# An mLSTM stage re-laid: outputs' pool at the other end of SBUF, more buffers, the first head's keys read in place, the next head's weights split ahead of the output gate

## The chip, the cores and the metric

One core of a Trainium2 chip runs the whole layer in one launch. The metric is the device time of an execution in microseconds (us); runs of one kernel are compared by their median. TensorE (PE) does the matmuls, VectorE (DVE) and ScalarE (ACT) the work on their results, GpSimd (POOL) some of it on SBUF, and SyncE (SP) issues most transfers. SBUF is shared by tiles that the program names; PSUM holds matmul results in banks.

## The reference

One layer of a diffusion backbone on 1024 latent tokens and 256 context tokens, width 1024. Only the part that matters here:

```python
h, hc = modulated RMS norms of x and ctx
aq, ak, av, mq, mk, mv, mo, mg, ga, gm = split_in_proj(h @ w_in)      # and the same of hc
att = windowed_gqa(q, k, v, k_ctx, v_ctx, sink)                       # branch B, 16 heads
ht = mlstm_bidirectional(mq, mk, mv, gates, ...context...)            # branch A, 4 heads
#   per head, chunks of 128 tokens, both directions (context first):
#   C = decay*C + (k*wk)^T v ;  h = (S v + q C*w) / max(|nq|, exp(-m)),  S = (q k^T)*exp(dmat)
ml = rms_norm(ht, norm_w) * sigmoid(mo)
y = (sigmoid(ga) * (att @ w_ba) + sigmoid(gm) * (ml @ w_bm)) @ w_out
x = x_mid + g2 * conv_ffn(norm(x_mid))
```

## The kernel before, in words

The work has four stages, one after another: start-up (modulation, context projections, `hT`, the normalized tokens transposed), attention with the branch gates, the mLSTM, and the tail (branch products, output projection, ConvFFN). Matmuls are made from fp16 or fp32r pieces: an operand is split into a high and a low half (`split_from`: ACT writes the high half, DVE the rest), and three products are summed (`mm3`, lines L163 to L165). Weights are scaled first: their squares are summed on ACT, added up by a small matmul with ones (L119), turned into a factor on POOL (L121, L122), and then split (`split_from`).

**Order of the work.** Each engine, and each engine's queue of transfers, runs its instructions in a fixed order. In attention the order is written out by hand (`tc.manual_schedule()`); elsewhere a planner orders the instructions of each engine by program order, by its own costs and by when it thinks that buffers come free. Work of a later stage is moved up into an earlier one where its inputs and its buffers allow. `tc.issue_after(x)` puts an instruction behind x on x's engine. Pools lie in SBUF as two stacks, one from each end (`side="right"` is the upper end); with `reuse_waits="tile"` a tile waits only for the earlier tiles that lay in its own bytes.

**End of attention.** In the last iterations PE makes the first mLSTM head's key and value products of the eight latent blocks (`early`), and `early_act` copies each from PSUM to `E.kv0[j]` (128x384, fp32, in the pool `kv0` at the upper end). POOL splits the weights of the first head there.

**mLSTM.** `prepare(h)` loads and squares head h's two weights, `load_kv(h)` splits the key/value weight (`whkv` on ACT, `wlkv` on DVE, L56). `proj_kv(h)` makes k and v of ten blocks (two of the context from DRAM tiles `vr`, eight of latent tokens): ACT copies the key (`k`), writes the value's high half (`VH`) and squares all 384 columns with an accumulator (`kvj`, L1325, into `sq`), DVE writes `VL`. `trans_k` transposes the keys on PE (`kT`, L1370) and splits them (`kh`, `kl`). `proj_q` does the queries (`qh`, `ql`, `qj`). `states(h)` turns the sum of squares into a scale (`mlq`, L1435), and updates the states of both directions: `kwh` on POOL, `kwl` on DVE, the product `dC` on PE, the sum `C` on DVE. `masked` adds the masks to the gate rows (`ub`, L1414; POOL for the first head, DVE for others), `decays` takes their exponentials on ACT (L1424). `core(h)` makes S, scales it by `ub` (L1485), splits it (`sh`, `sl`), and then per chunk and direction the outputs `o` and `i`, which go through `nm` (L1503 to L1508) into `hf`. `proj_o(h)` makes the output gate's products (`mo`, `sg`), `readout(h)` the norm, `turn(h)` transposes `hf` (`mt`, L1548), gates it and stores it (`mlT_d`, L1551). `branch_sums` prepares sums of tail weights (`s_ba` and others) in tiles of the outputs' pool `rp`.

The pool `rp` (`sg`, `hf`, `mo`, `kvj`, `qj`, about 22 KB of each partition) is the last of the lower stack. The tail opens its pools over the same lower stack from its bottom up; the first operands of the branch products are the weights `bawr` and the attention outputs `baar` (L1745), split into `bawh`, `bawl`, `baah`, `baal`. The gate rows `sga` (L1776) lie at the upper end.

The order of the calls in `stage_mlstm`:

```python
load_kv(0); proj_q(0); proj_kv(0)
E.kvx.close()
trans_k(0); states(0); masked(0); decays(0, nullcontext())
for _ in range(2): branch_sums()
for h in range(MLH):
    core(h); proj_o(h); readout(h)
    if h + 1 < MLH:
        prepare(h + 1); load_kv(h + 1); masked(h + 1)
        proj_kv(h + 1); trans_k(h + 1); proj_q(h + 1); states(h + 1)
```

Of the kernel before, what the change touches and what calls it, by code (L numbers as in the profile page):

```python
# [8 lines left out]
F32 = mybir.dt.float32  # L9
F32R = mybir.dt.float32r  # L10
F16 = mybir.dt.float16
BF16 = mybir.dt.bfloat16
AF = mybir.ActivationFunctionType
# [5 lines left out]
P = 128  # L19
# [6 lines left out]
NCB = NCTX // P  # L26
NBLK = NT // P
# [4 lines left out]
DQK = 128  # L32
# [13 lines left out]
def copy_act(nc, out, in_, scale=1.0):  # L46
    return nc.scalar.activation(out, in_, AF.Copy, scale=scale)  # L47
# [124 lines left out]
@with_exitstack  # L172
def layer_kernel(ctx: ExitStack, tc: tile.TileContext, A: dict, out: bass.AP, dbg=None):
    nc = tc.nc
    dbg = dbg or {}

    cp = ctx.enter_context(tc.tile_pool(name="cp", bufs=1, reuse_waits="tile"))
    dr = ctx.enter_context(tc.tile_pool(name="dr", bufs=1, space=DRAM, reuse_waits="tile"))

    ident = cp.tile([P, P], F32, name="ident")  # L180
    nc.sync.dma_start(ident, A["ident"])
    expo = cp.tile([P, 16], F32, name="expo")
    nc.gpsimd.memset(expo, -0.5)

    attT_d = dr.tile([D, L], F32, name="attT_d")
    mlT_d = dr.tile([D, L], F32, name="mlT_d")
    sga_d = dr.tile([D, L], F32, name="sga_d")
    sgm_d = dr.tile([D, L], F32, name="sgm_d")


    vecT = cp.tile([P, 256], F32, name="vecT")
    V_C, V_N1, V_N2, V_BM, V_CB, V_CW = 0, 16, 24, 32, 80, 124
    mods = cp.tile([P, 4, KT], F32, name="mods")
    m2 = cp.tile([P, 3, KT], F32, name="m2")
    g_d = [dr.tile([1, D], F32, name=f"g{i}_d") for i in range(2)]
    sil = cp.tile([P, KT, 2], F32, name="sil")

    psx = ExitStack()
    ps1 = psx.enter_context(tc.tile_pool(name="ps_mm", bufs=2, space=PSUM, reuse_waits="tile"))
    psx_t, psx_s = ExitStack(), ExitStack()  # L200
    banks = {}

    def turn_banks(n):
        psx_s.close()
        psx_t.close()
        banks["tp"] = psx_t.enter_context(tc.tile_pool(name=f"ps_tp{n}", bufs=n, space=PSUM, reuse_waits="tile"))

    def score_banks(n):
        banks["s"] = psx_s.enter_context(tc.tile_pool(name=f"ps_s{n}", bufs=n, space=PSUM, reuse_waits="tile"))

    turn_banks(3)
    score_banks(1)
    ph1 = ExitStack()
    hp = ph1.enter_context(tc.tile_pool(name="hTp", bufs=1, reuse_waits="tile"))
    hH = [hp.tile([P, L], F16, name=f"hH{k}") for k in range(KT)]
    hL = [hp.tile([P, L], F16, name=f"hL{k}") for k in range(KT)]
    hT = list(zip(hH, hL))
    gtile = hp.tile([P, NBLK, 16], F32, name="gtile")
    gb = hp.tile([P, 16], F32, name="gb")

    def mm_tile(name):
        return ps1.tile([P, 512], F32, tag="mm", name=name)

    def fl_tile(name):
        return ps1.tile([P, 512], F32, tag="fl", name=name, bufs=1)

    def tp_tile(name):
        return banks["tp"].tile([P, 512], F32, tag="tp", name=name)

    def s_tile(name):  # L230
        return banks["s"].tile([P, 1024], F32, tag="s", name=name)

    kx_d = dr.tile([NCB, P, MLH * DQK], F32, name="kx_d")
    vx_d = dr.tile([NCB, P, MLH * DV], F32, name="vx_d")
    E = Ctx()
    E.__dict__.update(
        nc=nc, tc=tc, A=A, ident=ident, expo=expo, vecT=vecT, mods=mods, m2=m2, g_d=g_d, maccs={}, hT=hT, gtile=gtile, gb=gb, dr=dr, out=out,
        attT_d=attT_d, mlT_d=mlT_d, sga_d=sga_d, sgm_d=sgm_d, kx_d=kx_d, vx_d=vx_d, sil3=sil, sil=sil[:, :, 0], dbg=dbg,
        mm_tile=mm_tile, fl_tile=fl_tile, tp_tile=tp_tile, s_tile=s_tile, psx_s=psx_s, turn_banks=turn_banks, score_banks=score_banks,
    )  # L240
    E.ones = cp.tile([P, P], F32, name="ones")
    nc.gpsimd.memset(E.ones, 1.0)
    E.hs = cp.tile([P, 2], F32, name="hs")
    E.w2 = ScaledWeights(E, tc, ph1)
    with ExitStack() as st:
        at = attention_setup(E, st)
        stage_startup(E, at)
        if dbg.get("stop") != "hT":
            stage_attention(E, st, at)
    if "attT" in dbg:  # L250
        dump(nc, tc, attT_d, dbg["attT"])
    if "sga" in dbg:
        dump(nc, tc, sga_d, dbg["sga"])
        dump(nc, tc, sgm_d, dbg["sgm"])
    if dbg.get("stop") in ("hT", "att"):
        ph1.close()
        psx_t.close()
        psx.close()
        return
    with ExitStack() as st:  # L260
        stage_mlstm(E, st)
    if "mlT" in dbg:
        dump(nc, tc, mlT_d, dbg["mlT"])
    E.gcx.close()
    ph1.close()
    if dbg.get("stop") == "ml":
        psx_t.close()
        psx.close()
        return
    with ExitStack() as st:  # L270
        stage_tail(E, st)
    psx_t.close()
    psx.close()
# [344 lines left out]
def stage_attention(E, st, at):  # L618
    nc, tc, A, ident, expo, hT = E.nc, E.tc, E.A, E.ident, E.expo, E.hT
# [13 lines left out]
    gc = E.gcx.enter_context(tc.tile_pool(name="gc", bufs=1, side="right", reuse_waits="tile"))  # L633
    E.kvp = E.kvx.enter_context(tc.tile_pool(name="kv0", bufs=1, side="right", reuse_waits="tile"))
    E.kv0 = {}
    norm_d = E.dr.tile([NKV * NB, 512], F32, name="norm_d")
    shift = wp.tile([P, 1], F32, name="shift", bufs=1)
    nc.gpsimd.memset(shift, PSHIFT)
# [464 lines left out]
    def early_act(j, ps):  # L1103
        E.kv0[j] = E.kvp.tile([P, 384], F32, name=f"kv0_{j}")
        copy_act(nc, E.kv0[j], ps[:, :384], scale=2.0 ** -15)

    def gate_slots(c):
        return [2 * c - 6, 2 * c - 5], [max(2 * c - 4, 0), max(2 * c - 3, 0)], 2 * c - 2, [2 * c - 1, 2 * c]
# [143 lines left out]
def stage_mlstm(E, st):  # L1252
# [5 lines left out]
    psd = E.psx_s.enter_context(tc.tile_pool(name="ps_d", bufs=2, space=PSUM, reuse_waits="tile"))  # L1258
    E.d_tile = lambda name: psd.tile([P, 512], F32, tag="d", name=name)
    mp = st.enter_context(tc.tile_pool(name="ml1", bufs=1, reuse_waits="tile"))  # L1260
    kp = st.enter_context(tc.tile_pool(name="mlk", bufs=13, reuse_waits="tile"))
    vp = st.enter_context(tc.tile_pool(name="mlv", bufs=13, reuse_waits="tile"))
    cp = st.enter_context(tc.tile_pool(name="mlc", bufs=2, reuse_waits="tile"))

    mlw = mp.tile([P, 2 * MLH], F32, name="mlw")
# [25 lines left out]
    def prepare(h):  # L1291
        H.setdefault(h, {})
        if h == 0:
            H[h].update(w_ml=E.wml0, w_mlqo=E.wqo0)
        for nm, pool in (("w_ml", None), ("w_mlqo", rwp))[: 2 * h]:
            H[h][nm] = w2.prepare(A[nm][h], 384, f"{nm}{h}", tp_tile(f"wt{nm}{h}"), pool)
        f, fq = H[h]["w_ml"][1], H[h]["w_mlqo"][1]
        c = H[h]["c"] = cp.tile([P, 8], F32, tag="c", name=f"mlc{h}")
        root = 2.0 ** -15
        nc.gpsimd.tensor_scalar(c[:, 0:1], f[:, 2:3], E.hs[:, 0:1], 2.0 ** -15, op0=ALU.mult, op1=ALU.mult)  # L1300
        nc.gpsimd.tensor_scalar(c[:, 1:2], c[:, 0:1], c[:, 0:1], EPS / ONE ** 2, op0=ALU.mult, op1=ALU.mult)
        nc.gpsimd.tensor_scalar(c[:, 2:3], f[:, 2:3], E.hs[:, 0:1], root * ONE * DQK ** 0.5, op0=ALU.mult, op1=ALU.mult)
        nc.gpsimd.tensor_scalar(c[:, 3:4], fq[:, 2:3], E.hs[:, 0:1], root, op0=ALU.mult, op1=ALU.mult)
        nc.gpsimd.tensor_tensor(c[:, 4:5], c[:, 2:3], c[:, 3:4], op=ALU.mult)
        H[h]["sq"] = cp.tile([P, NBLK + 2], F32, tag="sq", name=f"mlq{h}")

    def load_kv(h):
        raws, f = H[h].pop("w_ml")
# [9 lines left out]
    def proj_kv(h):  # L1318
# [6 lines left out]
            nc.scalar.activation(junk, src, AF.Square, scale=scale, accum_out=q[:, j : j + 1])  # L1325

        for j in orders(h)[0][1]:
            k = kp.tile([P, DQK], F32, tag="k", name=f"k{h}_{j}")
            if j < NCB:
                kv = kp.tile([P, DQK + DV], F32, tag="vr", name=f"vr{h}_{j}", bufs=2)  # L1330
                nc.sync.dma_start(kv[:, 0:DQK], E.kx_d[j][:, h * DQK : (h + 1) * DQK])
# [4 lines left out]
            else:  # L1336
                src, scale = mm_tile(f"kv{h}_{j}"), 2.0 ** -15
                mm3(nc, src[:, :384], hT, w, sl((j - NCB) * P, P), sl(0, 384))
            kc = copy_act(nc, k, src[:, 0:DQK], scale=scale)
            vs[j] = v_tiles(h, j, src[:, 128:384], None if scale == 1.0 else scale)  # L1340
            square(j, src[:, :384], scale)
            ks[j] = k
            if h:
                at = (2, 3)
# [237 lines left out]

    rwp = st.enter_context(tc.tile_pool(name="mlr4", bufs=4, reuse_waits="tile"))
    prepare(0)
    bp = st.enter_context(tc.tile_pool(name="mlb", bufs=15, reuse_waits="tile"))
    wp = st.enter_context(tc.tile_pool(name="mlw", bufs=2, reuse_waits="tile"))
    rp = st.enter_context(tc.tile_pool(name="mlr", bufs=2, reuse_waits="tile"))
    load_kv(0)
    proj_q(0)
    proj_kv(0)  # L1590
    E.kvx.close()
    trans_k(0)
    states(0)
    masked(0)
# [2 lines left out]
        branch_sums()  # L1597
    for h in range(MLH):
        core(h)
        proj_o(h)  # L1600
        readout(h)
        if h + 1 < MLH:
            prepare(h + 1)
            load_kv(h + 1)
        if h + 1 < MLH:
            masked(h + 1)
        if h + 1 < MLH:
            proj_kv(h + 1)
            trans_k(h + 1)
            proj_q(h + 1)  # L1610
            states(h + 1)
        if h == MLH - 1:
            turn(h)
        if h + 1 < MLH:
            for _ in range((3, 4, 3)[h]):
                branch_sums()
# [848 lines left out]
```

## Time and profile before

| | us |
|---|---|
| median of 3 runs (lowest, highest) | 1867.3 (1866.87, 1867.41) |
| the profiled execution: its time, its span | 1868.29, 1866.2 |
| PE busy in the span | 1783.6 (96%) |
| DVE, ACT, POOL busy | 1428.2, 1098.6, 533.9 |
| mLSTM stage (613 to 970 us of the span): PE busy of 357 us | 323.14 |

The page's rows give busy time per engine, the granted PE clock by slices (`PEclk`) and groups of instructions; answers of the trace give stretches (windows), waits by their releaser, and single instructions with their start, duration, engine, line, output and inputs, and in brackets the idle time before them and what ended it.

### The profile page before, as it was taken

Reading aid. Unit: us, or ns where it says so; the run is one execution under the profiler, and the core shown is the slowest. Engines: PE = TensorE matmul, PEld = TensorE weight load, DVE = VectorE, ACT = ScalarE, POOL = GpSimd, SP = SyncE. Lnnn points to the kernel's source line nnn. Section 1 sums busy time; section 2 is a strip of 40 time slices with the busy share of each in tenths; the row PEclk is TensorE's granted clock in tenths of the full one; section 3 lists DMA queues with packets and bytes.
Section 4 is the critical chain, followed back from the end, with each engine's and each line's share of the span. In section 5 each row is a group of like instructions: output and inputs, shape, how many; then the busy total and the mean of one; then the engine's idle time right before and its main releaser. Section 6 shows DMA issues by size and latency. Waiting matters only on the chain.

```text
span 1866.2 us, 27945 instructions
## 1 busy us (share of the span) xinstructions
PE 1783.6 (96%) x9215; PEld 1258.1 (67%) x9215; DVE 1428.2 (77%) x2876; ACT 1098.6 (59%) x2333; POOL 533.9 (29%) x767
## 2 busy tenths in 40 slices
PE   7989999999998898989979999999999999999999
PEld 3855555555554455545548887878888888888887
DVE  3848888888787676758577787688988898896665
ACT  4847777878786775656446663375544444465441
POOL 2477768686853641414020021000000000000000
PEclk9999999999999899999999999999999999999999
DMA  9747989878797544350428935412455444599751
GB/s 344 241 128 154 192 168 179 196 174 194 151 189 158 180 149 143 103 198 26 147 75 336 385 118 204 180 68 104 177 192 197 173 174 158 192 322 370 266 169 68
DMA packets 302193, 342.47 MB, mean 184 GB/s; under 512 B 176208, under 2 KB 200672, under 8 KB 299232
## 3 DMA queue, kind: packets, MB, share of 16 engines
q1 hardware_dynamic: 287648, 314.47, 55.6%
q10 hardware_dynamic: 14400, 26.22, 4.4%
q8 instruction: 72, 1.18, 0.3%
q14 instruction: 73, 0.60, 0.1%
HBM read 224.61 MB, written 76.16 MB: 161 GB/s over the span
## 4 chain that ended last, share of the span: by engine, by line
PE 77%; DVE 8%; ACT 4%; DMA 4%; POOL 4%; issue 3%; SPq 0%; POOLq 0%; ACTq 0%; DVEq 0%
PE g L706 8%; PE pq L706 6%; PE pa L2043 4%; PE pa L2044 4%; PE pa L2045 4%; PE po L706 3%; PE yb L2043 2%; PE yb L2044 2%; PE yb L2045 2%; PE dx L2043 2%; PE dx L2045 2%; PE dx L2044 2%; PE pb L2044 2%; PE pb L2045 2%; PE pb L2043 2%
## 5 line engine op out<-in xcount | busy, mean ns | idle before, releaser
L850 DVE CUSTOM_DVE_ANT_0 s<-s,maskA,nsink 128x640 f32<-128x640 f32 (+1 forms) x128 | 117.5, 918 | 74.3 <-PE s L845 73.8
L866 DVE TENSOR_TENSOR P<-s,P 128x640 f16<-128x640 f32 (+1 forms) x128 | 100.7, 786 | 1.0 <-ACT s L861 1.0
L860 ACT ACTIVATE P<-s,st 128x640 f16<-128x640 f32 (+1 forms) x128 | 98.3, 768 | 4.6 <-ACT st L858 0.3
L706 PE MATMUL g<-hH,fh 128*128 128x512 f16 x256 | 98.2, 384 | 0.0
L706 PE MATMUL g<-hL,fh 128*128 128x512 f16 x256 | 97.8, 382 | 0.0
L706 PE MATMUL g<-hH,fl 128*128 128x512 f16 x256 | 97.8, 382 | 0.0
L1449 POOL TENSOR_SCALAR kwh<-k,gcall 128x128 f16<-128x128 f32 x72 | 44.6, 623 | 175.7 <-PE dC L164 82.0
L861 ACT ACTIVATE s<-s,st 128x640 f32<-128x640 f32 (+1 forms) x128 | 93.9, 734 | 0.0
L706 PEld LDWEIGHTS <-hH 128*128 128x128 f16 x640 | 62.2, 98 | 36.4 <-DVE t L770 0.3
L858 ACT ACTIVATE st<-st,shift 128x1 f32<-128x1 f32 x128 | 37.6, 294 | 83.0 <-DVE st L850 82.3
L706 PE MATMUL pq<-wha,hH 128*128 128x384 f16 (+1 forms) x256 | 83.9, 328 | 0.0
L706 PE MATMUL pq<-wha,hL 128*128 128x384 f16 (+1 forms) x256 | 83.9, 328 | 0.0
L706 PE MATMUL pq<-wla,hH 128*128 128x384 f16 (+1 forms) x256 | 83.9, 328 | 0.0
L706 PEld LDWEIGHTS <-fh 128*128 128x128 f16 x512 | 48.3, 99 | 47.9 <-issue 1.7
L2181 ACT ACTIVATE cv<-ua,vecT 128x1024 f32<-128x1024 f32 x22 | 27.4, 1246 | 85.2 <-DVE ua L2154 85.2
L47 ACT ACTIVATE dfh<-drf 128x512 fp32r<-128x512 f32 x55 | 34.3, 628 | 58.3 <-PE dy L2044 26.2
L2043 PE MATMUL dx<-dwh,dfh 128*128 128x512 f32 (+1 forms) x176 | 68.3, 388 | 0.0
L2045 PE MATMUL dx<-dwh,dfl 128*128 128x512 f32 (+1 forms) x176 | 68.3, 388 | 0.0
L2044 PE MATMUL dx<-dwl,dfh 128*128 128x512 f32 (+1 forms) x176 | 68.2, 387 | 0.0
L163 PE MATMUL kv<-whkv,hH 128*128 128x384 f16 x192 | 63.1, 329 | 4.7 <-ACT kvj L1325 4.7
L164 PE MATMUL kv<-wlkv,hH 128*128 128x384 f16 x192 | 63.3, 330 | 4.4 <-DVE wlkv L56 4.4
L54 DVE TENSOR_TENSOR dfl<-drf,dfh 128x512 fp32r<-128x512 f32 x55 | 37.8, 691 | 36.0 <-ACT dfh L47 35.8
(706 smaller groups left out, 6210.8 us busy)
## 6 DMA issues: line engine op xcount, KB each, us to landing
ur<-in_w_up SPq DMA_DIRECT2D x22, 1024.0 KB
wmb<-in_w_modB SPq DMA_DIRECT2D x48, 256.0 KB
f_d<-cv SPq DMA_DIRECT2D x22, 512.0 KB
wm<-in_w_modA SPq DMA_DIRECT2D x16, 512.0 KB
fr<-in_w_g SPq DMA_DIRECT2D x32, 256.0 KB
drf<-fs_d SPq DMA_DIRECT2D x15, 512.0 KB
drw<-wt_d SPq DMA_DIRECT2D x14, 512.0 KB
w1b<-in_w_cx SPq DMA_DIRECT2D x16, 388.0 KB
```

Source lines behind the costliest of these rows:

```text
L54: rest = nc.vector.tensor_tensor(lo, src, whole, op=ALU.subtract)
L163: nc.tensor.matmul(ps, lh[:, ls], rh[:, rs], start=start and i == 0, stop=False)
L164: nc.tensor.matmul(ps, lh[:, ls], rl[:, rs], start=False, stop=False)
L706: nc.tensor.matmul(self.ps, x, w, start=self.i == 0, stop=self.i == self.n - 1)
L850: nc.vector.tensor_tensor_reduce(e, e, self.mask, scale=self.ss[:, h : h + 1], scalar=nsink[:, hh : hh + 1], op0=ALU.add, op1=ALU.min, acc ...
L860: nc.scalar.activation(two[:, :W], e, AF.Exp, bias=m, scale=-1.0)
L861: nc.scalar.activation(e, e, AF.Exp, bias=m, scale=-1.0, accum_out=st4[:, 4 + h : 5 + h])
L866: nc.vector.tensor_tensor(two[:, W : 2 * W], self.e[h], two[:, :W], op=ALU.subtract)
L1449: E.kw = nc.gpsimd.tensor_scalar(kh, ks[c], wk, 1.0, op0=ALU.mult, op1=ALU.mult)
L2043: nc.tensor.matmul(ps, lh, rh, start=start and i == 0, stop=False, skip_group_check=True)
L2044: nc.tensor.matmul(ps, lh, rl, start=False, stop=False, skip_group_check=True)
L2045: nc.tensor.matmul(ps, ll, rh, start=False, stop=stop and i == n - 1, skip_group_check=True)
```

## The change

1. `early_act`, in attention, also squares each product of the first head out of PSUM, with an accumulator (`E.kvq`, in the pool of gate columns); `proj_kv(0)` no longer squares them.
2. `proj_kv(0)` no longer copies the eight latent keys: the key tile is the slice `E.kv0[...][:, 0:128]`. The pool `kv0` stays open to the end of the stage.
3. The pool `rp` is opened at the upper end, below `kv0`.
4. More buffers: keys 13 to 16, values 13 to 20 (of `VH` and of `VL`), the 128x512 fp16 tiles 15 to 24.
5. `prepare(h + 1)` and `load_kv(h + 1)` stand ahead of `proj_o(h)` and `readout(h)` in program order.

```diff
@@ layer_kernel
+    E.kvx.close()
     E.gcx.close()
@@ stage_attention
+    E.kvq = gc.tile([P, NBLK + 2], F32, name="kvq")
 def early_act(j, ps):
         copy_act(nc, E.kv0[j], ps[:, :384], scale=2.0 ** -15)
+        junk = wp.tile([P, 320], F32, tag="sq", name=f"kvj{j}", bufs=1).bitcast(BF16)[:, :384]
+        nc.scalar.activation(junk, ps[:, :384], AF.Square, scale=2.0 ** -15, accum_out=E.kvq[:, NCB + j : NCB + j + 1])
@@ stage_mlstm
-    kp = ... bufs=13    vp = ... bufs=13
+    kp = ... bufs=16    vp = ... bufs=20
-        H[h]["sq"] = cp.tile(...)
+        H[h]["sq"] = cp.tile(...) if h else E.kvq
@@ proj_kv
-            k = kp.tile([P, DQK], F32, tag="k", name=f"k{h}_{j}")
+            first = h == 0 and j >= NCB
+            k = E.kv0[j - NCB][:, 0:DQK] if first else kp.tile([P, DQK], F32, tag="k", name=f"k{h}_{j}")
...
-            kc = copy_act(nc, k, src[:, 0:DQK], scale=scale)
+            if not first:
+                kc = copy_act(nc, k, src[:, 0:DQK], scale=scale)
...
-            square(j, src[:, :384], scale)
+            if not first:
+                square(j, src[:, :384], scale)
@@ pools and order
-    bp = ... bufs=15
+    bp = ... bufs=24
-    rp = ... bufs=2
+    rp = ... bufs=2, side="right"
     proj_kv(0)
-    E.kvx.close()
     for h in range(MLH):
         core(h)
-        proj_o(h)
-        readout(h)
         if h + 1 < MLH:
             prepare(h + 1)
             load_kv(h + 1)
+        proj_o(h)
+        readout(h)
```

More of the change, by code (lines that the diff above doesn't have):

```diff
@@ L1260, in stage_mlstm @@
     mp = st.enter_context(tc.tile_pool(name="ml1", bufs=1, reuse_waits="tile"))
-    kp = st.enter_context(tc.tile_pool(name="mlk", bufs=13, reuse_waits="tile"))
-    vp = st.enter_context(tc.tile_pool(name="mlv", bufs=13, reuse_waits="tile"))
+    kp = st.enter_context(tc.tile_pool(name="mlk", bufs=16, reuse_waits="tile"))
+    vp = st.enter_context(tc.tile_pool(name="mlv", bufs=20, reuse_waits="tile"))
     cp = st.enter_context(tc.tile_pool(name="mlc", bufs=2, reuse_waits="tile"))
@@ L1304, in prepare @@
         nc.gpsimd.tensor_tensor(c[:, 4:5], c[:, 2:3], c[:, 3:4], op=ALU.mult)
-        H[h]["sq"] = cp.tile([P, NBLK + 2], F32, tag="sq", name=f"mlq{h}")
+        H[h]["sq"] = cp.tile([P, NBLK + 2], F32, tag="sq", name=f"mlq{h}") if h else E.kvq
     def load_kv(h):
@@ L1338, in proj_kv @@
                 mm3(nc, src[:, :384], hT, w, sl((j - NCB) * P, P), sl(0, 384))
-            kc = copy_act(nc, k, src[:, 0:DQK], scale=scale)
-            vs[j] = v_tiles(h, j, src[:, 128:384], None if scale == 1.0 else scale)
-            square(j, src[:, :384], scale)
+            if not first:
+                kc = copy_act(nc, k, src[:, 0:DQK], scale=scale)
+            vs[j] = v_tiles(h, j, src[:, 128:384], None if first else scale)
+            if not first:
+                square(j, src[:, :384], scale)
             ks[j] = k
@@ L1584, in stage_mlstm @@
     prepare(0)
-    bp = st.enter_context(tc.tile_pool(name="mlb", bufs=15, reuse_waits="tile"))
+    bp = st.enter_context(tc.tile_pool(name="mlb", bufs=24, reuse_waits="tile"))
     wp = st.enter_context(tc.tile_pool(name="mlw", bufs=2, reuse_waits="tile"))
-    rp = st.enter_context(tc.tile_pool(name="mlr", bufs=2, reuse_waits="tile"))
+    rp = st.enter_context(tc.tile_pool(name="mlr", bufs=2, side="right", reuse_waits="tile"))
     load_kv(0)
```

## The prediction

> **What bounds the kernel now.** I read the page's totals first, then stretches of time per engine (windows: start and end in us, length, then busy time and instructions of each engine, granted PE clock, DMA share, GB/s), then PE's waits between 605 and 975 us (total us, count, longest).
>
> ```profile
> span 1866.2 us, 27945 instructions
> PE 1783.6 (96%) x9215; PEld 1258.1 (67%) x9215; DVE 1428.2 (77%) x2876; ACT 1098.6 (59%) x2333; POOL 533.9 (29%) x767
> ```
> ```profile
> 613.00:970.00 357.00, 323.14 (x1961) 190.63 (x1959) 258.09 (x737) 220.29 (x565) 111.06 (x248) 0.96 0.37 122
> 623.00:642.00 19.00, 11.07 (x61) 7.19 (x60) 14.66 (x34) 14.34 (x48) 8.86 (x17) 0.64 0.50 166
> 642.00:679.00 37.00, 36.62 (x233) 22.18 (x232) 31.72 (x124) 26.05 (x64) 15.08 (x38) 1.00 0.28 87
> 967.00:979.00 12.00, 1.95 (x16) 1.51 (x14) 5.51 (x9) 3.61 (x7) 0.00 (x0) 0.71 0.69 224
> 1000.00:1866.00 866.00, 860.96 (x3834) 710.53 (x3832) 695.81 (x983) 419.61 (x659) 24.88 (x20) 1.00 0.55 199
> ```
> ```profile
> PE kv L163 <- ACT kvj L1325: 4.7, 5, 1.6
> PE kT L1370 <- ACT k L47: 4.0, 3, 2.8
> PE kv L164 <- DVE wlkv L56: 4.4, 3, 1.5
> ```
>
> PE is the bound: 96% over all, and 860.96 of 866 us in the tail, where the change takes no matmul away. So only PE's idle time and its slow clock can be won: in the mLSTM stage 357 − 323.14 = 33.9 us idle, and at its end 12 − 1.95 = 10 us more. The largest hole is 623 to 642: 19 − 11.07 = 7.9 us idle, and the work in it ran at a granted clock of 0.64. The change touches that hole, the three waits for `wlkv` between heads, and the layout that the tail opens over. I cost these three and then what attention pays.
>
> **A. First head: keys in place, squares gone.** ACT and PE in order of time (start, duration, engine, line, output and inputs, idle time before):
>
> ```profile
> 620.00 0.30 ACT L47 ACTIVATE k<-kv 128x128 f32<-128x128 f32 x1
> 620.20 0.40 ACT L47 ACTIVATE VH<-kv 128x256 f16<-128x256 f32 x1
> 620.51 0.51 ACT L1325 ACTIVATE kvj<-kv 128x384 bf16<-128x384 f32 x1
> 620.92 0.19 ACT L1325 ACTIVATION_READ_ACCUMULATOR kvj<-kv 128x1 f32 x1
> 621.02 0.58 ACT L47 ACTIVATE qh<-q 128x512 f16<-128x512 f32 x1
> 626.27 0.33 PE L1370 MATMUL kT<-ident,k 128*128 128x128 f32 x1 [2.81 <-ACT k L47]
> 628.55 0.42 PE L163 MATMUL dC<-VH,kwh 128*128 128x258 f16 x1
> 629.29 0.37 POOL L1449 TENSOR_SCALAR kwh<-k,gcall 128x128 f16<-128x128 f32 x1 [6.27 <-PE dC L164]
> 629.62 5.36 POOL L1414 TENSOR_TENSOR ub<-ub,mlmask 128x512 f32<-128x512 f32 x4
> ```
>
> Each of the eight latent blocks costs ACT 621.02 − 620.00 = 1.02 us. Of it stays `VH`, 620.51 − 620.20 = 0.31; `k`, the square and its accumulator go: 0.71 × 8 = 5.7 us of ACT. Two of these chains matter. PE's transposes `kT` wait for the copied keys (4.0 us in three waits), and `dC` stands behind them on PE; POOL's `kwh` waits 6.27 us for `dC`, and behind it on POOL stand the four additions to `ub` (5.36 us), without which the core's first outputs can't start. With the keys there since attention, `dC` may run up to 628.55 − 622.8 = 5.7 us sooner, as the last block's values would then be the last thing needed; POOL's chain follows by at most its 6.27. Bounds: 0, if POOL's chain is held elsewhere; and the hole closes entirely, 19 us less the 11.07 of PE work brought to full clock (11.07 × 0.64 = 7.1), −11.9. I take **−6.0**, between the 5.7 of ACT and the 6.27 of POOL. Next in line is then DVE, 14.66 us busy of 19, so its idle 4.3 is a narrower limit if its work can't begin sooner (a rival below).
>
> The Trainium skill, "TensorE: Matmul & The Clock Gate", section "Part 1: The HAM clock gate", says that the clock halves after an idle window of about 3.4 us. Here 0.64 was granted although the longest single wait for a key was 2.81 us, so a gap as long as the Trainium skill's page asks for isn't what slowed this hole: the row disagrees. By the Trainium skill's rule closing shorter gaps would bring no clock, the far bound would be 19 − 11.07 = 7.9 instead of 11.9, and the sum would not change.
>
> **B. Next weights split ahead of the output gate.** The boundaries of heads, on PE, DVE and ACT:
>
> ```profile
> 677.74 0.28 PE L119 MATMUL wtw_ml<-wqw_ml,ones 128*128 128x4 f32 x2
> 680.95 2.57 ACT L47 ACTIVATE whkv<-wrw_ml,wfw_ml 128x768 f16<-128x768 f32 x3
> 681.42 3.80 DVE L56 SCALAR_TENSOR_TENSOR wlkv<-wrw_ml,wfw_ml,whkv 128x768 f16<-128x768 f32 x4
> 682.48 0.32 PE L164 MATMUL kv<-wlkv,hH 128*128 128x384 f16 x1 [1.45 <-DVE wlkv L56]
> 876.69 0.53 PE L165 MATMUL kv<-whkv,hL 128*128 128x384 f16 x1
> 879.86 0.33 PE L164 MATMUL kv<-wlkv,hH 128*128 128x384 f16 x1
> ```
>
> The sum of squares (L119) reaches PE only at 677.74, the split starts 3.2 us later, and PE catches up with it at 682.48. The new program order puts these steps ahead of `proj_o`, so they can run while PE makes `mo`. They add no work: DVE's 3.80 and ACT's 2.57 plus one more piece move into 642 to 679, where DVE has 37 − 31.72 = 5.3 us free and ACT 37 − 26.05 = 11. Ends: 0, when the planner leaves them where they were or the DVE split then delays the `nm` chain by as much; and −5.6, all of the 4.4 us of waits and the slow stretch that follows the third (876.69 to 879.86, 3.17 us at 0.53 for work that takes 0.33: 1.2). I take **−4.4**: the waits are the nearest rows. If DVE's free 5.3 us isn't contiguous, the `o` and `i` matmuls wait instead.
>
> **C. The outputs' pool at the upper end, and the tail's start.** SP's queue, ACT's and PE's starts, and the gate loads:
>
> ```profile
> 919.74 37.85 SPq L1745 DMA_DIRECT2D bawr<-in_w_ba  x2
> 968.09 4.00 SPq L1551 DMA_DIRECT2D mlT_d<-mo  x4
> 972.21 1.44 SPq L1745 DMA_DIRECT2D baar<-attT_d  x3
> 970.26 1.41 DVE L1550 SCALAR_TENSOR_TENSOR mo<-mt,mlw,sg 128x512 f32<-128x512 f32 x2 [0.34 <-DMA mlT_d<-mo]
> 978.14 3.73 ACT L47 ACTIVATE baah<-baar 128x512 fp32r<-128x512 f32 x6 [2.52 <-DMA baar<-attT_d]
> 978.82 0.79 PE L2043 MATMUL yb<-baah,bawh 128*128 128x512 f32 x1 [10.05 <-ACT baah L47]
> 645.21 0.36 ACTq L1776 DMA_DIRECT2D sga<-sga_d  x1
> 979.00:1000.00 21.00, 21.00 (x86) 16.95 (x87) 15.71 (x25) 17.07 (x32) 0.00 (x0) 0.92 0.94 373
> ```
>
> PE is idle for 10.05 us because `baar` is issued at 972.21 behind the four `mlT_d` stores, which wait on SP for DVE's `mo`; everything on SP behind a store waits with it. From the tile sizes the new layout gives: `baar`'s second tile no longer lies on `hf` but on a `ub` that is free by about 933; the first stays over 128x512 tiles. That helps only if the planner now issues `baar` ahead of the stores. The best case is that the bytes are there when DVE leaves `mo`, 970.26 + 1.41 = 971.67, and PE starts 978.82 − 978.14 = 0.68 later: 972.35, −6.5. The other way, the first `bawr` (issued at 919.74 before) now lies over values of the last head and small columns in use until about 964, so it can come late: 512 KB at the 373 GB/s of the row 979 to 1000 is 1.4 us, plus one split of 3.73 / 6 = 0.6: 2.0. And `sga`, loaded from 645.21 on, now lies on `hf` and `mo` of the last head; 1 MB at 373 GB/s is 2.8. So +4.8 at worst. The stores' order comes from the program, which is unchanged, and `mo` has two buffers as before; I take a third of the gain, **−2.0**.
>
> **D. Squares in attention.** Per tile of `kvj` (count, least/median/greatest ns), and attention's last stretches:
>
> ```profile
> L1325 ACT ACTIVATE kvj<-kv x32: 471/491/515, 619.5 to 911.0; 128x384 bf16<-128x384 f32 x32
> L1325 ACT ACTIVATION_READ_ACCUMULATOR kvj<-kv x32: 188/194/212, 619.9 to 911.4; 128x1 f32 x32
> 560.00:590.00 30.00, 28.18 (x179) 16.50 (x177) 25.34 (x71) 22.23 (x55) 10.13 (x9) 1.00 0.61 124
> 590.00:613.00 23.00, 18.78 (x98) 10.11 (x98) 12.09 (x21) 7.12 (x18) 13.04 (x12) 0.85 0.99 217
> ```
>
> Eight squares at the pitch of the rows above, 621.02 − 620.51 = 0.51, add 4.1 us to ACT, whose order there is written by hand, and hold the PSUM bank of each product that much longer. ACT is idle 7.8 of 30 us and 15.9 of 23, which covers them on average; where the softmax stands behind one, it waits 0.51. Bounds 0 and +4.1; I take **+1.0**, near the covered end.
>
> **E. More buffers.** More values, keys and 128x512 tiles: they let POOL's and DVE's splits run further ahead. No wait of PE in the rows above is for a buffer of theirs, so 0; the 4.7 us of `kv` behind `kvj` are PSUM reads and stay. If the extra room lets something run too early, that is the slower rival.
>
> **Sum.** −6.0 − 4.4 − 2.0 + 1.0 = −11.4. The profiled execution took 1868.29 us for its span of 1866.2; 1854.8 of span. The median of the runs is 1867.3, 1.0 below the profiled one: 1867.3 − 11.4 = 1855.9, so **1856**.
>
> **The rivals.**
> 1. *More is won* : the hole closes to half way between −6 and −11.9 (−9), the boundaries give all 5.6, and `baar` comes ahead of the stores (−6.5), +1: −20.1, 1847. For it: PE starts at 978.82 without needing `mo`. Against: the stores stand in program order.
> 2. *DVE takes over* : in 623 to 642 only DVE's idle 4.3 goes, the boundaries lose half to `nm` (−2), the tail stays, +1: −5.3, 1862. For it: DVE 14.66 of 19 and 31.72 of 37.
> 3. *No change* : A and B are won (−10.4), but the tail's operands come 4.8 late and attention pays all of 4.1: −1.5, 1866. Or the planner puts the splits behind `mo` again and B does not do what it says.
> 4. *Slower* : the outputs' pool now lies on bytes that nothing uses in attention, so the sums for the tail that stand in its tiles can be moved up into attention:
>
> ```profile
> 616.45 0.69 DVE L1567 TENSOR_TENSOR s_ba<-s_ba,s_ba 128x512 f32<-128x512 f32 x1 [9.05 <-DMA s_ba<-in_w_ba]
> 480.00:530.00 50.00, 49.75 (x300) 28.20 (x299) 40.41 (x106) 38.99 (x99) 44.09 (x46) 1.00 0.79 156
> ```
>
> Now DVE stood 9.05 us for their load in a stretch where little hung on it. In attention PE is busy 49.75 of 50 and waits for DVE's softmax at once; DVE runs in order, so everything behind the sum waits. Two sets of 9.05 are 18.1, less 11.4: +6.7, 1874. It makes the kernel slower by more than 0.2% from 11.4 + 3.7 = 15.1 us of exposed wait. Against it: DVE has 9.6 us of slack in 50, and a load issued early enough costs nothing.
>
> **How the numbers follow.** Forecast 0.42, rival 1 0.14, rival 2 0.17, rival 3 0.12, rival 4 0.15. 0.2% (3.7 us) is about what a measurement of this kernel can tell from no change: 1863.6 to 1871.0 counts as the same. Forecast, rival 1 and most of rival 2 are faster (0.70; 0.03 of rival 2 lies above 1863.6), rival 3 and that rest the same (0.15), rival 4 slower (0.15). The range leaves out rival 4: from 1845, a little below rival 1, to 1868, above rival 3. The likeliest case's own range is 1850 to 1861.
>
> **What the changed profile would show.** A: no `k` copies and `kvj` of the first head after 613, POOL's `kwh` released some 6 us sooner after the stage's start, PE busier than 11.07 of 19 before the first `o`. B: no PE row waiting for `wlkv`, and L119 ahead of the `mo` products. C: PE's wait before the first `yb` under 10.05. D: `kvj` squares among 560 to 613 and PE's idle there unchanged within 1. E: no `s_ba` before the end of attention. The prediction is wrong if the chain of PE's waits after 613 has a new owner of over 4 us, or if attention's end moves by more than 4.

## The result, and the profile after

The change made the kernel slower: 1876.69 us against 1868.21, medians of 20 runs each; the ratio is 1.0037, 95% interval [1.0025, 1.0049], about +6.9 us. (The ratio is worked out from all the runs; that of the two medians alone would be 1.0045.) The forecast of 1856 was wrong in sign, and the time lies outside its range of 1845 to 1868. The slower rival's 1874, or +6.7, came near the number by luck: what it described did not happen, as shown below. Runs of one kernel lie some 13 us apart (1868.43 to 1881.86 for the changed one). One profiled execution can lie 3 to 5 us off its kernel's median (1879.71 us for the changed one, 1866.86 against 1863.29 for e8), so below, a difference of single profiles under about 3 us carries nothing by itself. The profiled execution of the changed kernel has 11.7 us more span than that of before. All ratios are to the kernel before, run on the same chip.

The page's totals, then PE's waits between 590 and 1000 us (total us, count, longest):

```profile
span 1877.9 us, 27940 instructions
PE 1786.3 (95%) x9215; PEld 1256.5 (67%) x9215; DVE 1427.5 (76%) x2876; ACT 1095.7 (58%) x2325; POOL 529.8 (28%) x767
```
```profile
PE kv L163 <- ACT kvj L1329: 9.4, 6, 4.2
PE mt L1555 <- DVE hf L1547: 7.8, 3, 3.0
PE S L165 <- DVE kl L54: 7.7, 1, 7.7
PE q L163 <- DVE o L1238: 4.7, 1, 4.7
PE yb L2049 <- ACT bawh L47: 2.9, 1, 2.9
PE kT L1377 <- ACT k L47: 0.2, 1, 0.2
```

The waits that the change was aimed at are gone: `kT` for `k` fell from 4.0 us to 0.2, `kv` for `wlkv` from 4.4 to nothing, the tail's 10.05 to 2.9. Three new ones stand in their place (`mt`, `S`, `q`: 20.2 us), and `kv` behind `kvj` doubled. So the prediction's own sign of being wrong, a new owner of over 4 us among PE's waits, came three times. Where on the way it was lost shows from the start of the first PE instruction of some kinds (us of the span, from the timelines; the last column is the changed kernel without part 5, below):

| first of | before | after | without part 5 |
|---|---|---|---|
| `q`, first head | 612.13 | 608.60 | 606.40 |
| `o`, first head | 642.23 | 647.54 | 642.67 |
| `mlq`, second head | 730.89 | 742.14 | 731.69 |
| `mlq`, third head | 825.70 | 843.67 | 830.67 |
| `mlq`, fourth head | 923.41 | 941.46 | 928.05 |
| `yb`, tail | 978.82 | 987.74 | 976.53 |
| end | 1866.2 | 1877.9 | 1865.1 |

Attention ended 3.5 us sooner. From the first `q` to `o` the first head took 38.9 us instead of 30.1, from there to the second head's `mlq` 94.6 instead of 88.7, from the second to the third 101.5 instead of 94.8. The stretch from the fourth `mlq` to the tail's first `yb` got 9.1 us shorter, of which 2.8 were lost again behind it. The sum is 11.7.

**The first head.** The changed kernel's timeline, engine by engine in the order of cause (start, duration, engine, line, output and inputs, idle time before):

```profile
616.88 0.84 ACT L112 ACTIVATE wjw_ml<-wrw_ml 128x768 bf16<-128x768 f32 x1 [1.79 <-DMA wrw_ml<-in_w_ml]
617.84 0.59 ACT L47 ACTIVATE o<-po 64x512 f32<-64x512 f32 x1
618.46 0.68 DVE L1238 TENSOR_TENSOR o<-po,o 64x512 f32<-64x512 f32 x1 [2.92 <-ACT o L47]
619.20 0.59 PE L163 MATMUL q<-hH,wha 128*128 128x512 f16 x1 [4.73 <-DVE o L1238]
619.23 1.64 POOL L912 TENSOR_TENSOR o<-o,R 64x512 f32<-64x512 f32 x1 [5.85 <-DVE o L1238]
620.86 0.42 POOL L1304 TENSOR_SCALAR mlc<-wfa,hs 128x1 f32<-128x1 f32 x1
627.50 1.10 POOL L1456 TENSOR_SCALAR kwh<-k,gcall 128x128 f16<-128x128 f32 x3
629.92 5.63 POOL L1421 TENSOR_TENSOR ub<-ub,mlmask 128x512 f32<-128x512 f32 x4
629.72 6.45 DVE L54 TENSOR_TENSOR VL<-kv,VH 128x256 f16<-128x256 f32 x6
637.02 0.68 DVE L54 TENSOR_TENSOR kl<-kT,kh 128x512 f16<-128x512 f32 x1
637.76 0.29 PE L165 MATMUL S<-qh,kl 128*128 128x128 f16 x1 [7.68 <-DVE kl L54]
```

Attention's last outputs are done on PE at 608.6, but on ACT their copy stands behind a square of the second head's weights, which waits for its load. So `o` is copied at 617.84; DVE, PE's next PSUM bank and POOL wait for it. POOL, whose order now has `o` ahead of the small columns (`mlc`, and the ones and zeros of `VH` and `VL`), reaches its first `kwh` at 627.50. Then POOL's additions to `ub` and a row of `VL` on DVE run side by side, `VL` at 1.08 us each, and `kl` and `S` stand behind the row. The same in the kernel before, third and fourth square and the first `kwh`:

```profile
614.45 0.84 ACT L112 ACTIVATE wjw_ml<-wrw_ml 128x768 bf16<-128x768 f32 x1 [7.31 <-DMA wrw_ml<-in_w_ml]
619.99 0.38 POOL L1449 TENSOR_SCALAR kwh<-k,gcall 128x128 f16<-128x128 f32 x1
644.24 0.84 ACT L112 ACTIVATE wjw_ml<-wrw_ml 128x768 bf16<-128x768 f32 x1
```

There the third square was ahead of the copy too, but the fourth came 30 us later, and `kwh` 7.5 us sooner.

**The boundary of the first two heads**, in the changed kernel:

```profile
677.28 0.38 PE L119 MATMUL wtw_ml<-wqw_ml,ones 128*128 128x4 f32 x2
679.08 3.41 ACT L47 ACTIVATE whkv<-wrw_ml,wfw_ml 128x768 f16<-128x768 f32 x4 [0.30 <-POOL wfw_ml L122]
682.97 0.40 ACT L1542 ACTIVATE rj<-hf 128x256 f32<-128x256 f32 x1
686.74 1.25 DVE L1547 TENSOR_SCALAR hf<-hf,rr 128x256 f32<-128x256 f32 x4 [1.28 <-POOL rr L1544]
687.35 0.92 PE L1555 MATMUL mt<-ident,hf 128*128 128x128 f32 x6 [2.99 <-DVE hf L1547]
688.85 0.53 PE L164 MATMUL kv<-wlkv,hH 128*128 128x384 f16 x1
```

The splits are early enough that PE no longer waits for them, but they did not move where the prediction had put them. The squares that they need were done on ACT by 617.8, yet the planner has their sum (L119) on PE only at 677.28, behind most of `mo` (644.39 to 683.50). The splits therefore run from 679.08 to 685.46 (the last piece on DVE), beside the norm of the old head. On ACT they stand ahead of `rj`, the squares of the norm; POOL, which has the new head's small scales ahead of `rr`, reaches that at 684.69; DVE's `hf` follows. PE has the transposes `mt` of the old head ahead of most of the new head's `kv`. So PE waits 2.99 us for the old head where it had waited 1.45 for the new one, and the `kv` that follow run at 0.53 us in place of 0.33.

### The profile page after: what moved, and what is told of

Read it like the earlier page. It is cut to its first block, busy times and chain, and to the rows that moved or that the text cites. A ratio compares the mean times of both kernels' runs of the same rounds, so it can differ in the third digit from the quotient of the medians.

```text
span 1877.9 us, 27940 instructions
## 1 busy us (share of the span) xinstructions
PE 1786.3 (95%) x9215; PEld 1256.5 (67%) x9215; DVE 1427.5 (76%) x2876; ACT 1095.7 (58%) x2325; POOL 529.8 (28%) x767
## 4 chain that ended last, share of the span: by engine, by line
PE 69%; DVE 11%; DMA 7%; ACT 4%; POOL 4%; issue 3%; SPq 0%; ACTq 0%; POOLq 0%; DVEq 0%
PE g L708 8%; PE pq L708 5%; PE pa L2049 4%; PE pa L2050 4%; PE pa L2051 4%; PE po L708 3%; PE yb L2051 2%; PE yb L2049 2%; PE yb L2050 2%; PE dx L2049 2%; PE dx L2051 2%; PE dx L2050 2%; PE pb L2050 2%; PE pb L2049 2%; PE pb L2051 2%
## 5 line engine op out<-in xcount | busy, mean ns | idle before, releaser
L1456 POOL TENSOR_SCALAR kwh<-k,gcall 128x128 f16<-128x128 f32 x58 | 28.3, 491 | 172.4 <-PE dC L164 99.8
L165 PE MATMUL kv<-whkv,hL 128*128 128x384 f16 x192 | 63.9, 333 | 0.0
```

The source lines that it names most:

```text
L165: nc.tensor.matmul(ps, ll[:, ls], rh[:, rs], start=False, stop=stop and i == n - 1)
```

## The experiments

| run | edit | ratio | 95% interval |
|---|---|---|---|
| the change | all five parts | 1.0037 | 1.0025 to 1.0049 |
| e1 | before + part 5 | 1.0021 | 1.0011 to 1.0031 |
| e2 | before + part 3 | 0.9986 | 0.9976 to 0.9996 |
| e3 | before + part 4 | 0.9991 | 0.9979 to 1.0004 |
| e4 | before + parts 1, 2 | 1.0017 | 1.0002 to 1.0032 |
| e16 | before + parts 3, 4 | 1.0030 | 1.0019 to 1.0041 |
| e8 | change − part 5 | 0.9979 | 0.9966 to 0.9993 |
| e13 | change, part 5 at the first boundary only | 1.0018 | 1.0005 to 1.0032 |
| e14 | change, part 5 at the other two only | 1.0017 | 1.0006 to 1.0027 |
| e11 | before + half of part 5 (`prepare` alone) | 1.0039 | 1.0022 to 1.0057 |
| e5 | change, squares behind the `o` copy | 0.9998 | 0.9985 to 1.0011 |
| e6 | change, `VL` behind `kl` | 1.0026 | 1.0016 to 1.0036 |
| e7 | change, additions to `ub` on DVE | 1.0027 | 1.0014 to 1.0040 |
| e9 | e5 − part 5 | 0.9977 | 0.9962 to 0.9993 |
| e10 | e9, `VL` behind `kl` | 0.9976 | 0.9961 to 0.9991 |
| e15 | e10, 13 buffers of values | 0.9991 | 0.9981 to 1.0000 |
| e12 | e16, squares behind the `o` copy | 1.0014 | 1.0000 to 1.0028 |

The theory tested ("order" below): what the edits save is real, but the planner draws every engine's order anew, and it is new orders that lose. The rival: the edited operations themselves cost more than forecast.

**Each part alone.** Part 5 is e1:

```diff
 core(h)
+if h + 1 < MLH: prepare(h + 1); load_kv(h + 1)
 proj_o(h); readout(h)
-if h + 1 < MLH: prepare(h + 1); load_kv(h + 1)
```

> The kernel before with part 5 alone (prepare and load_kv ahead of proj_o and readout). Theory 'order': the three waits for the split weights (4.4 us) and for mo (1.3) go, and three waits of the transposes for the normed hf take their place, about 7.8 in the changed kernel; the first head and the tail keep the old order: 1.001, +1 to +4 us. Theory 'prediction' (part B of it right, the loss lies elsewhere): -4 us, 0.998.

Its PE waits (590 to 1000 us):

```profile
PE yb L2043 <- ACT baah L47: 9.8, 1, 9.8
PE kv L163 <- ACT kvj L1325: 7.9, 7, 2.5
PE mt L1548 <- DVE hf L1540: 5.5, 3, 2.7
```

`wlkv` (4.4) and `mo` (1.3) are gone from the list, `hf` (5.5) is in it, and `kv` behind `kvj` grew from 4.7 to 7.9, while the tail still waits 9.8. So +3.9 us (interval 2.1 to 5.8): part 5 loses by itself.

Part 3 is e2 (`kv0` stays open as in the change, since it lies further out in the same stack):

```diff
-rp = ... name="mlr", bufs=2
+rp = ... name="mlr", bufs=2, side="right"
```

> The kernel before with part 3 alone (outputs' pool at the upper end; the pool of early keys stays open under it, as it must). Theory 'order': the two last squares of the next head's weights stand ahead of the last output copy on ACT, so PE waits 4 to 5 us for the bank before the queries of the first head; the first attention operands are issued ahead of the last stores, so the wait of 10.05 before the first branch product falls to about 3: together -2 us, 0.999. Theory 'prediction': no stall at the first queries, tail -2: 0.999 too, but with no wait there and still about 8 in the tail; the two waits tell them apart.

Both waits came out as the order theory said in kind: `yb` 2.5 us instead of 10.05, and `q` behind DVE `o` 2.5 us, half of the 4 to 5 expected; 0.9986. Part 4 is e3 (buffers 13 to 16, 13 to 20, 15 to 24):

> The kernel before with part 4 alone (more buffers). Theory 'order': more buffers shift the lower stack, so the first attention operands come free early and are issued ahead of the stores: the tail's wait of 10.05 falls to about 3, and no stall before the first queries: -5 to -7 us, 0.997. Theory 'prediction' (buffers cost and bring nothing): 1.000.

The tail's wait fell to 3.1 us here too, though the total moved by less than its interval, which excludes the order theory's 0.997. Against the tail's gain stands the first head: 34.4 us from `q` to `o` where the kernel before took 30.1. Parts 1 and 2 are e4:

> The kernel before with parts 1 and 2 alone (squares in attention, keys read in place). Theory 'order': VL of the latent blocks run on DVE in one row beside POOL's work, at 1.07 us in place of 0.41, ahead of kl; the saved 5.7 us of ACT are spent there: -3 to +3 us. Theory 'prediction': -6 + 1 = -5 us, 0.997. A third theory, that reading the keys in place or squaring in attention is itself the loss: +6 us or more, 1.003 and up.

The loss shows in one wait. PE waits of e4, and its timeline between 625 and 639:

```profile
PE dC L163 <- DVE C L1462: 13.3, 2, 12.2
```
```profile
625.86 5.50 POOL L1421 TENSOR_TENSOR ub<-ub,mlmask 128x512 f32<-128x512 f32 x4
625.95 5.69 DVE L54 TENSOR_TENSOR VL<-kv,VH 128x256 f16<-128x256 f32 x4
637.51 0.69 DVE L56 SCALAR_TENSOR_TENSOR ql<-q,qh 128x512 f16<-128x512 f32 x1 [3.07 <-ACT qh L47]
638.12 0.75 DVE L1462 COPY C<-dC 128x258 f32<-128x258 f32 x2
638.59 0.37 PE L163 MATMUL dC<-VH,kwh 128*128 128x258 f16 x1 [12.22 <-DVE C L1462]
```

With the keys there early, ACT makes `VH` in a row and DVE is given `VL` in a row; the copy of `dC` that frees PE's bank stands behind it. It also stands behind `ql`, for which DVE waits 3.07 us: ACT's `qh` comes behind four squares of the next head's weights (633.17 to 636.90). `kT` waits no more, and nothing is won. The +3.2 us (interval +0.4 to +6.0) speaks for the order theory in kind, just past the upper end of its −3 to +3, and against the prediction's −5. The interval just reaches the third theory's 1.003, but the squares in attention do not delay its end (`q` at 611.87 against 612.13).

**Part 5 taken out of the change.** e8 undoes the diff of e1:

> The changed kernel without part 5. Theory 'order': the waits of mt for hf (7.8) go, those for wlkv (4.4) and mo (1.3) return: 2 to 4 us less than the changed kernel, 1.0017 to 1.0026; the stall before the queries stays, since part 3 made it. Theory 'prediction': part 5 brought 4.4, so 1.006.

The step from 1.0037 to 0.9979 is 0.0058, or 10.8 us (by the two intervals, some 3 us either way); the order theory had said 2 to 4. PE's waits of e8:

```profile
PE S L165 <- DVE kl L54: 7.5, 1, 7.5
PE kv L163 <- ACT kvj L1329: 4.5, 4, 2.7
PE kv L164 <- DVE wlkv L56: 4.4, 3, 1.5
PE q L163 <- DVE o L1238: 2.6, 1, 2.6
```

The 7.5 us behind `kl` are still there, and the kernel is faster than before all the same: parts 1 to 4 together gain 0.2%. Which boundary loses was asked by e13 and e14:

```diff
-if h + 1 < MLH: prepare(h + 1); load_kv(h + 1)
+if h + 1 < MLH and h == 0: ...        # e13; e14: h > 0; the others stand behind readout(h)
```

> The changed kernel with part 5 at the first boundary only (head 1's weights early, the others as before). Theory 'boundary' (each boundary pays for the split ahead of the norm, about 2 us in three): 1.000, a third of the 10.8 us that part 5 costs there. Rival 'first head' (head 1's early weights reach back into the end of attention and the first head): nearly all of the loss, 1.003.

> The changed kernel with part 5 at the second and third boundary only. Theory 'boundary': two thirds of the loss, 1.002. Rival 'first head': 0.998 to 0.999, as without part 5.

From 0.9979, the first boundary alone costs 0.0039 (7.3 us) and the two others together 0.0038 (7.1): both halves lose, about as much as each other. That they add up to more than the whole lies within the intervals. So neither expectation was whole: the boundary theory was right for e14 and too low for e13. The rival's reach back into the first head doesn't show: in e13 the first head took 36.7 us from `q` to `o` (36.3 in e8), and the loss stands between that and the second head's `mlq`, 93.2 against 89.0. e11 tried half of it, `prepare` ahead and `load_kv` behind `readout`:

> The kernel before with half of part 5: only prepare (loads, squares and scale of the next head) ahead of the output gate, the split itself behind the norm. Theory 'order' (what part 5 lost is the split on ACT ahead of the norm's squares, and the transposes behind that): no wait of mt for hf over 1 us, the wait for wlkv shrinks: 0.998 to 0.999. Rival: the transposes wait for hf by 5.5 us as with the whole of part 5: 1.002.

It lost, 1.0039, and neither expectation held: the transposes wait, but for `mo`. With the scale early, DVE's order has the four pieces of `wlkv`, four `ub` and two `VL` ahead of `mo`, and the second half of the transposes waits for the bank that `mo` frees, three times:

```profile
PE mt L1548 <- DVE mo L1550: 7.7, 3, 2.6
PE kv L163 <- ACT kvj L1325: 6.9, 4, 2.9
```

In the kernel before, where the scale is late, all eight `hf` and the first two `mo` are through on DVE ahead of `wlkv` (673.05 to 681.42). So the splits on ACT ahead of `rj` are not the only way to lose here; splits that stay early but stand behind `rj` and `mo` were not tried.

**The orders of the first head.** e5 puts the third and fourth square of the second head's first weight behind the last `o` copy:

```diff
-copy_act(nc, o2, po[HD:P])
+E.last_o = copy_act(nc, o2, po[HD:P])
 ... in prepare, for head 1's w_ml, i > 1:
+with tc.issue_after(E.last_o.ins): self.square(q, i, raw, name)
```

> The changed kernel with one order mended: the third and fourth square of the next head's first weight stand behind the last output copy on ACT. Theory 'order': the wait of 4.7 us before the queries falls below 1; the row of VL on DVE behind it stays: 3 to 5 us less than the changed kernel if POOL's work starts sooner with it, 1.001 to 1.002 of the kernel before. Rival 'hidden': the late stage only waits elsewhere for the same weights: 1.0037 as before.

1.0037 became 0.9998: 7.3 us, more than the 3 to 5 expected. Two squares on one engine, in another order, are worth about as much as the whole loss. The copy runs at 608.76 instead of 617.84, no wait before `q` of over 1 us is left, and the wait behind `kl` is 3.7 instead of 7.7, since POOL starts sooner. e6 puts `VL` behind `kl`:

```diff
+trans_k(0) ahead of proj_kv(0)
+with tc.issue_after(E.kl.ins): vl = src - vh      # first head, latent blocks
```

> The changed kernel with VL of the eight latent blocks put behind the second half of kl on DVE (the transposes stand ahead of them in program order). Theory 'order': the 7.7 us wait of S for kl falls below 1 and VL, run beside less of POOL's work, cost less: 5 to 7 us less than the changed kernel, 1.000 to 1.001. Rival 'DVE bound': the outputs then wait for VL by as much, 1.0037.

The wait for `kl` is gone, but a step of 0.0011 is within the intervals, and the 1.000 to 1.001 of the order theory was missed. e7 puts the four additions to `ub` on DVE:

> The changed kernel with the four additions to ub of the first head on DVE in place of POOL. It tells what VL cost by themselves: if they run long because POOL works beside them, VL falls from 1.08 to about 0.41 us each (-5 us of DVE, +2.7 for the additions): 2 to 3 us less than the changed kernel, 1.002. If VL are long because they read the early products at the far end of SBUF, they stay at 1.08 and the time rises by 2.7: 1.005.

1.0027 lies in the intervals too, and its own interval excludes the 1.005 that slow `VL` would have given; what it and e15 show of `VL` is in the last section. e9 and e10 join the mends:

> The changed kernel without part 5 and with the two weight squares behind the last output copy on ACT (both edits that gained most). Theory 'order': the wait before the queries goes, 2 to 4 us less than without part 5 alone: 0.996 to 0.997. Rival 'one loss, counted twice' (each of the two edits only lets the same chain start sooner): no better than without part 5 alone, 0.998.

> The same, and VL of the eight latent blocks behind kl. Theory 'order': no wait of S for kl, first head at the forecast of the prediction's part A: 0.994 to 0.996, about -8 us. Rival 'DVE bound': the outputs wait for VL instead: as without this edit, 0.996 to 0.997.

Both came out as e8 (0.9979), far within their intervals. For e9 that is the rival's number, though the interval holds the order theory's 0.997 too. For e10 it excludes the order theory, but no wait of the outputs for `VL` shows either. e10 has no long wait left in the first head (the longest is 2.3 us, `dC` behind POOL's `kwh`) and goes from `q` to `o` in 29.5 us, where the kernel before took 30.1. So against the kernel before, the keys in place bring the first head nothing that can be measured even when all orders are mended. Whether POOL's small columns are the reason was e15 (the values' buffers 13 again in e10):

> The kernel with all three mends and 13 buffers of values again instead of 20. Theory 'POOL' (the first head is bound by POOL: with 20 buffers it writes 40 small columns of ones and zeros ahead of the first kwh in place of 26, at 0.12 us each): kwh and the first output 1.5 to 2 us sooner, 0.996 to 0.997. Rival: POOL is not the bound, or the tail loses its early operands: 0.998 or more.

`kwh` starts at 617.91 instead of 623.40, but most of that is an earlier end of attention: counted from `q` it is 12.0 us instead of 13.3. `o` comes no sooner after `q` (31.6 us), since DVE's order changed again (`dC` behind `C`: 7.9 us); 0.9991. The theory that POOL alone binds is not borne out.

**Parts 3 and 4 together.** e16, and e12 with the squares behind the copy:

> The kernel before with parts 3 and 4 alone, squares left where the planner puts them. If the two gains add: 0.9977. If they are the same gain (first operands of the tail early): 0.999. If moving the squares was the gain's end in the run of the pool and buffers: 0.998 here against 1.0014 there.

> The kernel before with parts 3 and 4 (outputs' pool at the upper end, more buffers) and the two weight squares behind the last output copy: a version with no part that lost. Theory 'order': the tail's 7 us, attention's end 3 us sooner, no stall before the queries: 0.995 to 0.997. Rival 'same gain twice' (parts 3 and 4 both free the first operand's bytes): 0.998 to 0.999, as either alone.

Neither expectation held. Each part alone was 0.999, together they are 1.0030. PE waits of e16:

```profile
PE q L163 <- DVE o L1235: 4.2, 1, 4.2
PE mt L1549 <- DVE wfw_ml L120: 3.4, 1, 3.4
PE yb L2043 <- ACT bawh L47: 3.1, 1, 3.1
```

The tail's gain is there (48.4 us from the fourth `mlq` to `yb`, 55.4 before). Most of what eats it is in the first head: 41.0 us from `q` to `o`, against 30.1 before, 34.1 in e2 and 34.4 in e3. The squares ahead of the copy are in it (4.2). The scale that comes late behind the transposes (3.4) is in e2 already (2.7). With the squares moved the kernel was at 1.0014; why the scale is late is not settled.

Parts 1 and 2 have another worth here. e8 is e16 with these two parts added, and e9 is e12 with them: 0.9979 against 1.0030, and 0.9977 against 1.0014. That is 9.5 and 6.9 us less (some 3 to 4 us either way), where alone they cost 3.2. The first head took 36.3 us instead of 41.0, and 33.6 instead of 37.0.

## Why the prediction was wrong, step by step

- **B failed, and with it the sign.** The step was "They add no work", with DVE's free 5.3 us and ACT's free 11 between 642 and 679 as the cover. Free time in a window isn't a free place in an order. The splits did not go into that window (679.08 to 685.46, and L119 stayed behind most of `mo`, against the sign that the prediction had named). Where they went, ACT has `rj` behind them, and DVE `hf` and `mo`, and PE wants those before the new head's products. The forecast was −4.4; part 5 measured +3.9 alone (e1) and +10.8 within the change (change against e8). The text named what would happen instead ("the `o` and `i` matmuls wait instead") but not the waiting `mt`. One reading was off too: "the split starts 3.2 us later" is the second piece of `whkv`; the first ran at 679.17, 1.4 us after the sum.
- **A was wrong.** The waits it priced went (`kT` 4.0 to 0.2), but the end of the first head wasn't set by them. "POOL's chain follows by at most its 6.27" took POOL's start as given; POOL started 7.5 us later, behind `o`, and DVE's `VL` became a row. −6.0 was forecast; parts 1 and 2 alone gave +3.2 (e4), and with the orders mended the head took 29.5 us against 30.1. On top of parts 3 and 4 they gained 9.5 and 6.9, of which the profiles show 4.7 and 3.4 in the first head, which those parts had made longer.
- **C was right in kind and mis-sized.** `baar` came ahead of the stores, as the best case had it. The stretch from the fourth `mlq` to `yb` shrank by 9.1 us, 2.8 came back behind it, against −2.0 forecast and −6.5 as the best end. A third of the gain was a bad choice between the ends: the planner did move the loads. What is left of PE's wait is for the weights (`bawh`, 2.9), which the prediction said could come 2.0 late. The total of part 3 alone, −2.6 (e2), meets the −2.0 by luck: the tail gained 7.7, and other stretches lost some of it again, the first head 4.0 (34.1 against 30.1). SP's queue after:

```profile
972.79 1.40 SPq L1751 DMA_DIRECT2D baar<-attT_d  x3
984.17 0.98 SPq L1558 DMA_DIRECT2D mlT_d<-mo  x2
```

- **D was right** as far as one profile can tell: attention didn't end later for the squares (`q` at 611.87 in e4, 612.13 before; +1.0 had been forecast).
- **E was priced at 0** as a matter of waits for buffers. Alone the buffers gave 0.9991, within its interval of 1; but that 0 is a gain less a loss. They moved `baar` ahead in e3, and POOL writes 22 pairs of small columns by 645 us where it wrote 15 (the `VH` row of each pair, after and before):

```profile
L1290 POOL CAST VH<-ones 128x2 f16<-128x2 f32 x22 | 4.1, 185 | 0.0
```
```profile
L1286 POOL CAST VH<-ones 128x2 f16<-128x2 f32 x15 | 4.2, 281 | 0.0
```

  In e3, 40 of these columns and `o` stand ahead of POOL's first `kwh`, which comes 15.5 us after the first `q`; before, 26 stood ahead of it, `o` behind, and it came after 7.9.

- **The slower rival was the wrong mechanism.** The sums for the tail did not go up into attention: the kernel before already had one set there, and the change moved it out. Before, then after:

```profile
593.30 0.69 DVE L1567 TENSOR_TENSOR s_ba<-s_ba,s_ba 128x512 f32<-128x512 f32 x1
```
```profile
613.39 0.69 DVE L1574 TENSOR_TENSOR s_ba<-s_ba,s_ba 128x512 f32<-128x512 f32 x1 [9.53 <-DMA s_ba<-in_w_ba]
```

  Attention's end came 3.5 us sooner with it (also in e2, 2.6). That doesn't make the sums the cause: in e3 they stayed in attention (590.94), and `q` came 3.8 us sooner all the same. The rival's +6.7 met the measured +6.9 by luck.
- **The sum itself** added five terms. The four groups measured alone add up to 1.0021 − 0.0014 − 0.0009 + 0.0017: 1.0015; together they are 1.0037, which the intervals don't tell apart from that. But parts 3 and 4, 0.9977 by addition, are 1.0030, and part 5 costs 3.9 us alone and 10.8 on top of parts 1 to 4 (0.9979). With a planner the terms don't add.

What stays open: why part 5 costs 10.8 us within the change and 3.9 alone, and why parts 3 and 4 together lose. Both look like interplays of several orders. The single profiles don't tell which wait is covered by which: e8 and e9 both wait over 7 us behind `kl`, only e8 waits before `q` (2.6), e10 does neither, and all three take the same time. The version to keep is the change without part 5: 0.9979, faster than both.

## What to carry to other kernels

Where a planner draws the orders, an early call is a new order on every engine: before pricing a moved step, ask what stands behind it on each engine that it uses, and who waits for that. Work that "has room" in a window can still stand ahead of the one instruction that the bound engine needs. When several edits come together, time each one left out of the whole as well as each alone: here part 5 cost 3.9 us by one reading and 10.8 by the other, and only the second showed that the rest was a gain; parts 1 and 2 cost 3.2 alone and gained 9.5 on top of parts 3 and 4.

## What the runs showed of the hardware

`VL` of the first head (both inputs in SBUF) takes 0.41 us without POOL's additions beside it and 1.08 with them, in the changed kernel. By shape between 600 and 645 us (count, busy us, mean ns, idle before), after, with the additions on DVE (e7), and where POOL's additions were over at 624.7 and `VL` ran from 630.8 on (e15):

```profile
L54 DVE TENSOR_TENSOR VL<-kv,VH 128x256 f16<-128x256 f32 x8 | 8.3, 1079 | 0.0
```
```profile
L54 DVE TENSOR_TENSOR VL<-kv,VH 128x256 f16<-128x256 f32 x8 | 3.9, 538 | 0.0
```
```profile
L1296 DVE TENSOR_TENSOR VL<-kv,VH 128x256 f16<-128x256 f32 x8 | 2.8, 415 | 0.0
```

So it isn't the place of the early products that costs, but the neighbour; the trace of before held both durations (0.42 at 628.57, 1.01 at 630.16, when the additions had begun), and the prediction did not use them. (In e7 seven of the eight took 0.41 or 0.42; the eighth took 1.41, beside POOL's `o`.) The other side can lose instead: in e7 a `kwh` of POOL, 0.37 to 0.40 us just before, is shown with 2.57 beside six `VL` in a row (629.12 to 631.21):

```profile
628.80 2.57 POOL L1456 TENSOR_SCALAR kwh<-k,gcall 128x128 f16<-128x128 f32 x1 [0.80 <-PE dC L164]
```

The Trainium skill, "SBUF — State Buffer", section "Who interferes with whom", says that a DVE instruction with two SBUF inputs contends with a GpSimd instruction that reads SBUF; these rows agree.

The granted clock fell around short waits. In the changed kernel, windows (start and end, length, busy time of PE, PEld, DVE, ACT and POOL, granted clock, DMA share, GB/s) around the 4.73 us before `q`, which began at 614.47, and behind the 2.99 before `mt`:

```profile
616.00:616.50 0.50, 0.00 (x0) 0.00 (x0) 0.00 (x0) 0.00 (x0) 0.00 (x0) 0.86 0.66 214
616.50:619.20 2.70, 0.00 (x0) 0.00 (x0) 0.74 (x2) 2.27 (x5) 0.00 (x0) 0.50 0.96 237
688.50:691.00 2.50, 2.50 (x10) 1.21 (x8) 1.29 (x3) 2.46 (x7) 2.42 (x2) 0.50 0.01 2
```

It was 1.00 until 616.00, 0.86 on average in the next half us and 0.50 from 616.50 on, so it fell some 1.9 us into the wait, and the `q` products ran at 0.63 us instead of 0.38 until 622.99, 3.8 us. During the wait before `mt` it was 1.00 throughout; it fell after PE had begun again, and `kv` ran at 0.53 us instead of 0.33 from 688.5 to 691.4. The Trainium skill, "TensorE: Matmul & The Clock Gate", section "Part 1: The HAM clock gate", gives about 3.4 us for the idle and the busy window. The 3.8 us until full clock are near its busy window; both falls came after less idle time than its rule asks for.
